# The first gate's modulation on TensorE in four column strips, and the condition spread by a DMA

## The chip, the cores and the metric

One core of a Trainium2 chip runs the whole kernel in one launch. The metric is device time in microseconds (us). The kernel before takes 2292.65 us, the median of three runs (2290.1, 2292.65 and 2293.73). The engines are called by their names or by the profile's: TensorE (PE for matmuls, PEld for weight loads), VectorE (DVE), ScalarE (ACT), GpSimd (POOL) and SyncE (SP), whose queue issues the DMAs here.

## What is computed

Two decoder layers over 256 tokens of 2048 features, all in f32. Each layer is a mixer (a recurrent block, then sparse attention) and a squared-ReLU MLP, so there are four sub-layers s = 0 to 3. Each sub-layer is modulated by a shift, a scale and a gate that come from one condition vector c:

```python
cond = jax.nn.silu(c)
mod = jnp.einsum('bd,jde->bje', cond, ada_w[layer]) + ada_b[layer]
shift, scale, gate = jnp.split(mod, 3, axis=-1)
h = x * (1.0 + scale[:, 0, None]) + shift[:, 0, None]
y = rglru_mixer(h, ...)
x = _layer_norm(DN_ALPHA * x + (1.0 + gate[:, 0, None]) * y, ln_w[layer, 0], ln_b[layer, 0])
```

For one sub-layer, shift, scale and gate are 2048 numbers each, and each is a product of cond (2048) with a 2048 x 2048 block of `ada_w`. The recurrent block projects h to 4096 columns (`lru_in`), applies a short convolution and a gelu, two block-diagonal gate products (`lru_gate`), a scan over the tokens, and an output projection (`lru_out`).

## The kernel before

**Stream of weights.** All large weights come from memory once, as units of 1 MB (128 partitions by 2048 f32) in one fixed order, through a ring of six raw slots (`RAW = 6`). `prefetch` (L95) issues one DMA per unit on SP's queue as soon as a slot is free; `pump` (L109) handles a unit when the builder's own clock says that it has landed (3 us a unit). A unit of kind "w" is split by ScalarE (L135) and VectorE (L136) into a high and a low part, in pieces of 512 columns, that lie in a ring of 16 pieces (`RING`); TensorE then makes each product with three matmuls (`mm3`, L193 to L195). A unit of kind "n" (`lru_gate`) is read by plain f32 matmuls directly from its raw slot (L840, in `gates`).

**Modulation.** A unit of kind "a" is a block of `ada_w` with 128 outputs on the partitions and 2048 inputs along them. VectorE multiplies it by cond and sums along the row in one instruction (L120), which gives 128 of the outputs as a column of `mods[s]`. There are 12 x 16 = 192 of them. For that cond stands on all partitions.

**The condition.** At the start c is loaded as two rows of 1024 on one partition (L291); ScalarE and VectorE make the silu (L314 to L316); a matmul with a column of ones (L319) spreads 512 columns at a time over the partitions, and VectorE copies them out of PSUM (L320).

**The gate.** Once the 16 gate units of a sub-layer are done, `make_gate` (L464) adds the bias and 1 (L466, L467), transposes the columns to rows on TensorE (L470), and stores 2048 numbers to memory (L474); `load_gate` (L477) later loads them onto all partitions. The projection's evacuation multiplies by it (L632).

**Order.** The builder lists the units by hand. The first stage interleaves shift and scale units of sub-layer 0 with the first part of `lru_in`. Then `merge` spreads 24 side units (16 gate units of sub-layer 0, 8 shift and scale units of sub-layer 1) evenly over 36 main units (4 `lru_gate`, 16 `lru_in`, 16 `lru_out`). Of what has been written down, a scheduler then puts each engine's instructions in order.

**PSUM.** Eight banks: four of kind "g" and four of kind "m". A group of `gates` takes two of each. Small tiles of 128 x 512 come from a pool of six (`t2`), larger ones from a pool of twenty (`t4`).

Of the kernel before, what the change touches and what calls it, by code (L numbers as in the profile page):

```python
# [9 lines left out]
F32 = mybir.dt.float32  # L10
# [8 lines left out]
D = 2048  # L19
# [8 lines left out]

C_ADA, C_LNW, C_LNB, C_CW, C_CB, C_GB, C_LAM, C_CMPB, C_N = 0, 192, 256, 320, 384, 400, 432, 448, 450

# [19 lines left out]
class Builder:  # L50
# [18 lines left out]

# [1 line left out]
    def t4(self, shape, dtype=F32):  # L71
# [13 lines left out]

# [1 line left out]
    def set_stream(self, items):  # L87
# [21 lines left out]
    def pump(self):  # L109
        nc = self.nc  # L110
        while self.pi < len(self.items):
            it = self.items[self.pi]
            if it.kind == "d":
                self.pi += 1
                continue
            if self.arrive[self.pi] > self.now:
                return
            r = it.raw
            if it.kind == "a":
                nc.vector.scalar_tensor_tensor(r, r, self.one, self.cond, op0=OP.mult, op1=OP.mult, accum_out=it.col)  # L120
            elif it.kind == "raw":
                if not it.run(r):
                    return
            elif it.kind == "n":
                if not it.done:
                    return
            else:
                w = min(1024, it.width)
                s = it.p0 + 2 * it.group
                if s + 2 > self.cons + RING:  # L130
                    return
                src = r[:, 1024 * it.group:1024 * it.group + w]
                hi = self.whi[:, s % RING:s % RING + 2, :].rearrange("p a b -> p (a b)")[:, :w]
                lo = self.wlo[:, s % RING:s % RING + 2, :].rearrange("p a b -> p (a b)")[:, :w]
                nc.scalar.activation(hi, src, AF.Copy)  # L135
                nc.vector.tensor_tensor(out=lo, in0=src, in1=hi.bitcast(F32), op=OP.subtract)  # L136
                self.prod = s + 2
                it.group += 1
                if 2 * it.group < it.pieces:
                    continue  # L140
            self.pi += 1
            self.inflight -= 1
            self.prefetch()
            if it.then:
                it.then()

# [1 line left out]
    def spawn(self, gen, delay=0.0):  # L148
# [28 lines left out]

# [1 line left out]
    def piece(self, i):  # L179
# [6 lines left out]
    def head(self, kind):  # L186
        """The unit that is next in the stream, as it came."""
        self.until(lambda: self.items[self.pi].kind == kind and not self.items[self.pi].done and self.arrive[self.pi] <= self.now)
        return self.items[self.pi], self.items[self.pi].raw
# [20 lines left out]
    def gemm_ws_outer(self, act, dones, kinds, groups):  # L210
        """Several chunks of columns side by side, a few tiles of the contraction at a time."""
        bs = [[self.bank([128, 2, 256], kind) for _ in range(2)] for kind in kinds]
# [13 lines left out]
    def gemm_as(self, act, done, stagger=None, kind="g"):  # L226
        b = [self.bank([128, 512], kind) for _ in range(2)]
        if not stagger:
# [10 lines left out]
            return  # L239
        # the first token tile runs ahead of the second by as many tiles of weights as the ring holds  # L240
        c0 = self.cons
# [16 lines left out]

# [1 line left out]
    def new_act(self):  # L260
# [17 lines left out]
def build(ctx, tc, a, out):  # L278
# [4 lines left out]

# [1 line left out]
    cond = const.tile([128, 2048], F32, name="cond")  # L285
    B.cond = cond
    B.one = const.tile([128, 1], F32, name="one")
    V.memset(B.one, 1.0)
    crow = B.t4([1, 1024]), B.t4([1, 1024])
    for h in range(2):  # L290
        nc.sync.dma_start(out=crow[h], in_=a["c"][1024 * h:1024 * h + 1024].rearrange("(o n) -> o n", o=1))  # L291
    cols = const.tile([128, C_N], F32, name="cols")
# [15 lines left out]

    # silu(c), on every partition
    ones = const.tile([1, 128], F32, name="ones")  # L310
    V.memset(ones, 1.0)
    for h in range(2):
        cx = B.t4([1, 1024])
        SC.activation(cx, crow[h], AF.Tanh, scale=0.5)  # L314
        V.tensor_scalar(cx, cx, 0.5, 0.5, op0=OP.mult, op1=OP.add)
        V.tensor_tensor(out=cx, in0=cx, in1=crow[h], op=OP.mult)  # L316
        for i in range(2):
            pc = B.bank([128, 512], "m")
            T.matmul(pc, ones, cx[:, 512 * i:512 * i + 512], start=True, stop=True)  # L319
            V.tensor_copy(cond[:, 1024 * h + 512 * i:1024 * h + 512 * i + 512], pc)  # L320

# [1 line left out]
    state = {}  # L323

    def ada_items(s, part, tiles=range(16), then=None):
# [32 lines left out]
    def x_item(g):  # L358
# [6 lines left out]
        return it  # L365

    stream = []
    def w_part(name, ix, k0, k1):
# [16 lines left out]

    stream += merge(lru_in + lru_out, ada_items(0, 2, then=hook(("gate", 0))) + ss_group(*GROUPS1[0]))
    for i, (k0, k1) in enumerate(GROUPS1):
# [29 lines left out]

# [1 line left out]
    def ln_cols(s):  # L419
        return cols[:, C_LNW + 16 * s:C_LNW + 16 * s + 16], cols[:, C_LNB + 16 * s:C_LNB + 16 * s + 16]  # L420

    def make_ss(s, k0=0, k1=16):
        """h = zn * hA + hB, with zn the normalized rows before sub-layer s (its input where s is 0)."""
        m = mods[s]
# [19 lines left out]
    def modulate(s, k0, k1, rows, A):  # L444
        """Up to four feature tiles of the transposed rows become the two parts of the modulated ones."""
        make_ss(s, k0, k1)
# [14 lines left out]

    gate_dram = [B.dram.tile([2048], F32, name=f"gate{s}") for s in range(4)]

# [29 lines left out]

# [1 line left out]
    def split(hi, lo, src):  # L495
        SC.activation(hi, src, AF.Copy)  # L496
        V.tensor_tensor(out=lo, in0=src, in1=hi.bitcast(F32), op=OP.subtract)  # L497

# [1 line left out]
    def residual_source(s):  # L500
# [4 lines left out]
    def ln_task(s, z, t, stats, A, fin=None, rows=None):  # L505
        """Normalizes the rows of token tile t and, with A, makes sub-layer s+1's modulated rows, transposed
        (or with rows, the transposed rows alone; or with fin, the last layer norm's w and b, the output)."""
        mv = B.small([128, 2], "mv")
# [79 lines left out]
    def residual_task(s, z):  # L588
        """The output of sub-layer s, zn w + b, goes to memory until the next layer norm."""
        for n in range(4):  # L590
            w, b = lnrow(s, n)
            yield 3.0
            w, b = (v.rearrange("p (o c) -> p o c", o=1).to_broadcast([128, 2, 512]) for v in (w, b))
            V.tensor_tensor(out=z[n], in0=z[n], in1=w, op=OP.mult)
            V.tensor_tensor(out=z[n], in0=z[n], in1=b, op=OP.add)
            nc.sync.dma_start(out=xd[s][n], in_=z[n])
            yield 1.3
# [4 lines left out]
    def proj(s, A_in, z, A_out, first=True, last=True, fin=None, rows=None, kinds="gggg"):  # L602
        """z += act @ W over four chunks of columns. The last part of a sub-layer applies the gate, adds the
        residual and normalizes."""
        act = B.act_as(A_in)
# [117 lines left out]

    # ================= layer 0: RG-LRU =================
    # softplus(-lambda) from a range-reduced exponential and the series of log1p
    sp2 = const.tile([128, 16], F32, name="sp2")
# [168 lines left out]

    # ================= MLP of layer 0 =================
    B.until(lambda: znT[3] is not None and znT[3][1] == 3)
# [4 lines left out]

    # ================= layer 1: sparse attention =================
    # relative bias by distance: row h, column 127 + distance
    oh = B.t4([33, 512])
# [4 lines left out]

    # compressed keys and values
    kc = const.tile([128, 4, 15], F32, name="kc")
# [4 lines left out]
    def compress(i):  # L917
        """Sixteen of the 32 positions in a block; the other sixteen come with the next unit."""
        j, h = divmod(i, 2)
# [89 lines left out]

    # branch gates  # L1010
    gbank = B.bank([128, 256], "g")
# [26 lines left out]

    # attention
    O = [None] * NK  # L1040
# [8 lines left out]
    def back(t, start, step, n, copies=None):  # L1049
        """The last axis of t walked backwards from start."""  # L1050
        dims = [list(d) for d in t.ap]
# [116 lines left out]

    # ================= MLP of layer 1 =================
    z_in = z  # L1170
# [25 lines left out]
def _layout(i):  # L1196
# [6 lines left out]
    cols = [_cols(f["ada_b"]), _cols(f["ln_w"]), _cols(f["ln_b"]), _cols(f["lru_conv_w"][0]), _cols(f["lru_conv_b"][0]),  # L1203
            _cols(f["lru_gate_b"][0]), _cols(f["lru_lambda"][0]), _cols(f["nsa_cmp_b1"][0])]
    r["cols"] = np.ascontiguousarray(np.concatenate(cols, axis=1))
    r["lnrow"] = np.ascontiguousarray(np.stack([f["ln_w"].reshape(4, D), f["ln_b"].reshape(4, D)], axis=1))
    r["lru_in"] = _units(f["lru_w_in"][0])
# [32 lines left out]
```

## Time and profile before

| | before |
|---|---|
| median of the runs | 2292.65 us |
| lowest and highest run | 2290.1 and 2293.73 us |
| span of the profiled execution | 2292.0 us |
| time of the profiled execution outside its span | none shown |
| TensorE busy | 2198.1 us, 96% |
| VectorE busy | 1672.3 us, 73% |
| ScalarE busy | 1057.2 us, 46% |
| read from memory | 613.30 MB |

The span is the time from the first to the last instruction of one profiled execution. An engine's busy time is the sum of its instructions' time; matmuls are pipelined and their ends are modelled, so spacing from start to start says more than busy time. In a row of the trace, "out<-in" names the tiles (without buffer numbers), and "xN" the number of instructions.

### The profile page before, as it was taken

To read this page: it belongs to the slowest core of one execution; us is meant where nothing else is said; L and a number is where in the kernel's file an instruction comes from. 1 tells how busy PE (TensorE), PEld (TensorE's weight loads), DVE (VectorE), ACT (ScalarE), POOL (GpSimd) and SP (SyncE) were. 2 spreads that over 40 slices of the span, in tenths; PEclk is the share of its full clock that TensorE was granted. 3 is DMA by queue.
4 is the path that set the end of the run, shared out by engine and by line. 5 is a ranking of instruction groups with operands and counts; after the bars stand their busy time and mean duration, and the time that the engine had idled before them with its cause. 6 is when DMAs were issued, how large, how long until landed. Compare 5 with 4: busy or idle time off the path is not lost.

```text
span 2292.0 us, 33881 instructions
## 1 busy us (share of the span) xinstructions
PE 2198.1 (96%) x13970; PEld 1966.2 (86%) x13970; DVE 1672.3 (73%) x1987; ACT 1057.2 (46%) x1383; POOL 0.2 (0%) x4
## 2 busy tenths in 40 slices
PE   4799998989999999999999999999999999999997
PEld 3798977978998998998789988788989989988986
DVE  8899999886777767778887688668766444454456
ACT  2356644364453453444443355536544534443541
POOL 0000000000000000000000000000000000000000
PEclk9899999999999999999999999999999999999999
DMA  9987888988878878788689775356788555555561
GB/s 371 411 331 286 338 328 322 373 346 341 306 302 321 298 273 310 294 302 319 234 292 349 293 272 214 132 192 219 281 308 307 190 190 189 191 184 185 208 250 37
DMA packets 98218, 623.95 MB, mean 272 GB/s; under 512 B 10909, under 2 KB 13405, under 8 KB 26896
## 3 DMA queue, kind: packets, MB, share of 16 engines
q1 hardware_dynamic: 98064, 621.80, 72.5%
q8 instruction: 109, 1.79, 0.3%
q14 instruction: 45, 0.37, 0.0%
HBM read 613.30 MB, written 8.45 MB: 271 GB/s over the span
## 4 chain that ended last, share of the span: by engine, by line
PE 84%; DVE 11%; ACT 2%; issue 2%; DMA 1%; DVEq 0%; SPq 0%; ACTq 0%
PE g L195 26%; PE g L194 26%; PE g L193 26%; DVE raw L120 5%; DVE wlo L136 2%; PE m L1124 1%; PE m L1090 1%; ACT whi L135 1%; DMA raw<-in_lru_in 1%; DVE s L801 1%; PE m L929 1%; PE m L1116 0%; PE m L1127 0%; DVE s L497 0%; ACT s L454 0%
## 5 line engine op out<-in xcount | busy, mean ns | idle before, releaser
L136 DVE TENSOR_TENSOR wlo<-raw,whi 128x1024 fp32r<-128x1024 f32 x721 | 872.1, 1222 | 512.4 <-ACT whi L135 510.9
L135 ACT ACTIVATE whi<-raw 128x1024 fp32r<-128x1024 f32 x721 | 754.7, 1057 | 911.7 <-PE g L195 454.2
L193 PE MATMUL g<-s,whi 128*128 128x256 f32 (+1 forms) x2768 | 781.1, 283 | 51.6 <-ACT s L496 50.0
L194 PE MATMUL g<-s,whi 128*128 128x256 f32 (+1 forms) x2768 | 780.4, 282 | 5.1 <-DVE s L497 5.1
L195 PE MATMUL g<-s,wlo 128*128 128x256 f32 (+1 forms) x2768 | 780.6, 283 | 3.2 <-DVE wlo L136 3.2
L193 PEld LDWEIGHTS g<-s,whi 128*128 128x128 f32 (+1 forms) x2768 | 523.1, 189 | 59.1 <-ACT s L496 53.0
L193 PE MATMUL g<-whi,s 128*128 128x512 f32 x1376 | 547.4, 398 | 5.4 <-ACT s L496 5.4
L194 PE MATMUL g<-wlo,s 128*128 128x512 f32 x1376 | 544.9, 396 | 0.0
L195 PE MATMUL g<-whi,s 128*128 128x512 f32 x1376 | 544.6, 396 | 0.3 <-DVE s L497 0.3
L194 PEld LDWEIGHTS g<-s,whi 128*128 128x128 f32 (+1 forms) x2768 | 525.8, 190 | 8.9 <-DVE s L497 6.8
L195 PEld LDWEIGHTS g<-s,wlo 128*128 128x128 f32 (+1 forms) x2768 | 525.1, 190 | 4.8 <-DVE wlo L136 3.8
L120 DVE SCALAR_TENSOR_TENSOR raw<-raw,one,cond 128x2048 f32<-128x2048 f32 x192 | 447.7, 2345 | 19.1 <-DMA raw<-in_ada 18.9
L193 PEld LDWEIGHTS g<-whi,s 128*128 128x128 f32 x1376 | 258.9, 188 | 70.2 <-ACT s L496 7.4
L195 PEld LDWEIGHTS g<-whi,s 128*128 128x128 f32 x1376 | 258.7, 188 | 64.8 <-DVE s L497 2.2
L194 PEld LDWEIGHTS g<-wlo,s 128*128 128x128 f32 x1376 | 258.9, 188 | 62.0 <-issue 0.8
L454 ACT ACTIVATE s<-s,hB,hA 128x256 f32<-128x256 f32 x32 | 16.7, 590 | 120.9 <-DVE hA L430 80.4
L194 PE MATMUL m<-s,whi 128*128 128x256 f32 x256 | 71.1, 278 | 0.0
L195 PE MATMUL m<-s,wlo 128*128 128x256 f32 x256 | 71.1, 278 | 0.0
L193 PE MATMUL m<-s,whi 128*128 128x256 f32 x256 | 70.8, 279 | 0.2 <-ACT whi L135 0.2
L497 DVE TENSOR_TENSOR s<-t,s 128x512 fp32r<-128x512 f32 x78 | 52.8, 685 | 1.5 <-ACT s L496 1.3
L675 ACT ACTIVATE t<-g 128x512 f32<-128x512 f32 x58 | 33.9, 588 | 34.7 <-PE g L195 34.7
L193 PEld LDWEIGHTS m<-s,whi 128*128 128x128 f32 x256 | 47.8, 188 | 0.5 <-ACT whi L135 0.4
(189 smaller groups left out, 1048.6 us busy)
## 6 DMA issues: line engine op xcount, KB each, us to landing
raw<-in_mlp_w SPq DMA_DIRECT2D x256, 1024.0 KB, 5.0
raw<-in_ada SPq DMA_DIRECT2D x192, 1024.0 KB, 6.6
raw<-in_lru_in SPq DMA_DIRECT2D x28, 1024.0 KB, 8.4
raw<-in_nsa_kv SPq DMA_DIRECT2D x24, 1024.0 KB, 5.3
raw<-in_lru_out SPq DMA_DIRECT2D x16, 1024.0 KB, 6.3
raw<-in_nsa_q SPq DMA_DIRECT2D x16, 1024.0 KB, 6.5
raw<-in_nsa_out SPq DMA_DIRECT2D x16, 1024.0 KB, 4.9
t<-in_lnrow SPq DMA_DIRECT2D x24, 256.0 KB, 6.2
```

The costliest lines, as they stand in the source:

```text
L120: nc.vector.scalar_tensor_tensor(r, r, self.one, self.cond, op0=OP.mult, op1=OP.mult, accum_out=it.col)
L135: nc.scalar.activation(hi, src, AF.Copy)
L136: nc.vector.tensor_tensor(out=lo, in0=src, in1=hi.bitcast(F32), op=OP.subtract)
L193: mm(out, lhi, rhi, start=start, stop=False, skip_group_check=True)
L194: mm(out, lhi, rlo, start=False, stop=False, skip_group_check=True)
L195: mm(out, llo, rhi, start=False, stop=stop, skip_group_check=True)
L497: V.tensor_tensor(out=lo, in0=src, in1=hi.bitcast(F32), op=OP.subtract)
L675: SC.activation(r2, banks[b], AF.Relu)
L801: V.scalar_tensor_tensor(o[:, sh:], p[:, :256 - sh], tap(i, j), o[:, sh:], op0=OP.mult, op1=OP.add)
L929: T.matmul(hv, r[:, 128 * l:128 * l + 128], x[:, :, h:15 + h, l], start=(h == 0 and l == 0), stop=(h == 1 and l == 15))
L1090: T.matmul(ps, qT[:, h, 128 * t:128 * t + 128], kT[g // 2][:, g % 2, :, 0:K], start=True, stop=True)
L1124: T.matmul(po, vt[br][:, kt, 128 * g:128 * g + 128], pT[:, br, kt], start=first, stop=False)
```

## The change

The 16 gate units of sub-layer 0 are replaced by 16 units of the same size in another layout: 128 of the inputs on the partitions, all 2048 outputs along them. Each is multiplied on TensorE straight from its raw slot by four f32 matmuls, whose weights are one column of the condition (`condT`, 128 x 16) and whose outputs are rows of 512 on partitions 0, 32, 64 and 96 of one PSUM bank, summed over the 16 units. Then VectorE adds 1 and the bias on these four partitions, and four DMAs store the gate. The gates of the other three sub-layers stay as they were. The condition is loaded by four DMAs that repeat 512 numbers on all 128 partitions, and its silu is made there, on 128 partitions; the matmuls with ones and the copies go. A second copy of c, with the inputs on the partitions, comes with the column constants (`cols`, 16 columns more).

```diff
-    crow = B.t4([1, 1024]), B.t4([1, 1024])
-    for h in range(2):
-        nc.sync.dma_start(out=crow[h], in_=a["c"][1024 * h:1024 * h + 1024].rearrange("(o n) -> o n", o=1))
+    cd = a["c"]
+    crow = [B.t2([128, 512]) for _ in range(4)]
+    for h in range(4):
+        nc.sync.dma_start(out=crow[h], in_=bass.AP(tensor=cd.tensor, offset=cd.offset + 512 * h, ap=[[0, 128], [1, 512]]))
...
-    ones = const.tile([1, 128], F32, name="ones")
-    V.memset(ones, 1.0)
-    for h in range(2):
-        cx = B.t4([1, 1024])
+    for h in range(4):
+        cx = cond[:, 512 * h:512 * h + 512]
         SC.activation(cx, crow[h], AF.Tanh, scale=0.5)
         V.tensor_scalar(cx, cx, 0.5, 0.5, op0=OP.mult, op1=OP.add)
         V.tensor_tensor(out=cx, in0=cx, in1=crow[h], op=OP.mult)
-        for i in range(2):
-            pc = B.bank([128, 512], "m")
-            T.matmul(pc, ones, cx[:, 512 * i:512 * i + 512], start=True, stop=True)
-            V.tensor_copy(cond[:, 1024 * h + 512 * i:1024 * h + 512 * i + 512], pc)
+    condT = const.tile([128, 16], F32, name="condT")
+    SC.activation(condT, cols[:, C_C:C_C + 16], AF.Tanh, scale=0.5)
+    V.tensor_scalar(condT, condT, 0.5, 0.5, op0=OP.mult, op1=OP.add)
+    V.tensor_tensor(out=condT, in0=condT, in1=cols[:, C_C:C_C + 16], op=OP.mult)
...
+    def gate0_items():
+        acc = []
+        def unit(k):
+            def run(r):
+                if not acc:
+                    acc.append(B.bank([128, 512], "m"))
+                for j in range(4):
+                    T.matmul(acc[0][32 * j:32 * j + 1, :], condT[:, k:k + 1], r[:, 512 * j:512 * j + 512], start=k == 0, stop=k == 15, skip_group_check=True)
+            it = Item("p", a["gate0"][k])
+            it.run = run
+            if k == 15:
+                it.then = lambda: B.spawn(rows())
+            return it
+        def rows():
+            acc_bias = B.t2([128, 512])
+            for j in range(4):
+                nc.sync.dma_start(out=acc_bias[32 * j:32 * j + 1, :], in_=a["gate0_b"][j:j + 1, :])
+            yield 3.0
+            for j in range(4):
+                sl = slice(32 * j, 32 * j + 1)
+                V.scalar_tensor_tensor(acc_bias[sl, :], acc[0][sl, :], 1.0, acc_bias[sl, :], op0=OP.add, op1=OP.add)
+                nc.sync.dma_start(out=gate_dram[0][512 * j:512 * j + 512].rearrange("(o n) -> o n", o=1), in_=acc_bias[sl, :])
+            state["gate", 0] = True
+        return [unit(k) for k in range(NK)]
...
-    stream += merge(lru_in + lru_out, ada_items(0, 2, then=hook(("gate", 0))) + ss_group(*GROUPS1[0]))
+    stream += merge(lru_in + lru_out, gate0_items() + ss_group(*GROUPS1[0]))
```

In `pump`, a unit of the new kind "p" runs its four matmuls when it has landed, in the place where kind "a" issued L120.

## Rows read from the trace of the kernel before

**Rows 1.** The page, part 1: busy time and share of the span.

```profile
PE 2198.1 (96%) x13970; PEld 1966.2 (86%) x13970; DVE 1672.3 (73%) x1987; ACT 1057.2 (46%) x1383; POOL 0.2 (0%) x4
```

**Rows 2.** Busy time by stretch: us, engines, then granted clock, DMA share, GB/s.

```profile
14.00:40.00 26.00, 0.80 (x2) 0.50 (x2) 22.61 (x39) 4.85 (x8) 0.00 (x0) 1.00 1.01 419
40.00:147.00 107.00, 90.25 (x707) 88.65 (x708) 97.36 (x102) 39.61 (x51) 0.00 (x0) 0.92 0.98 387
147.00:304.00 157.00, 150.69 (x1054) 141.02 (x1053) 155.54 (x185) 111.42 (x159) 0.00 (x0) 0.99 0.81 305
```

**Rows 3.** The chain of waits from 147 to 310 us, by line.

```profile
by line: issue 11.1%; DVE raw L120 9.3%; PE g L193 9.2%; PE g L195 9.1%; PE g L194 8.9%; DVE s L801 8.6%; DVE wlo L136 8.4%; DVE s L873 4.4%; DMA raw<-in_lru_out 3.9%; ACT s L850 2.4%; DVE s L870 2.2%; DVE s L868 2.2%; ACT whi L135 1.8%; DV
```

**Rows 4.** Waits of PE, 147 to 374 us: us in total, times, longest us.

```profile
PE g L195 <- DVE wlo L136: 3.2, 3, 2.4
...
PE g L193 <- ACT s L496: 1.4, 1, 1.4
PE g L193 <- ACT s L850: 1.1, 1, 1.1
PE g L193 <- ACT whi L135: 0.5, 1, 0.5
PE m L840 <- DVE s L801: 0.4, 1, 0.4
```

**Rows 5.** Groups of instructions, 147 to 304 us: busy us, mean ns, idle before.

```profile
L120 DVE SCALAR_TENSOR_TENSOR raw<-raw,one,cond 128x2048 f32<-128x2048 f32 x17 | 39.8, 2344 | 0.0
```

**Rows 6.** Timeline of DVE: the last gate unit, the first use of the gate.

```profile
289.24 2.35 DVE L120 SCALAR_TENSOR_TENSOR raw<-raw,one,cond 128x2048 f32<-128x2048 f32 x1
...
314.45 0.68 DVE L632 TENSOR_TENSOR s<-g,s 128x512 f32<-128x512 f32 x1
```

**Rows 7.** PE: timeline (start us, us), source L840 (ns min/median/max), groups by form.

```profile
215.03 1.89 PE L840 MATMUL g<-s,raw 128*128 128x256 f32 x8
...
L840 PE MATMUL g<-s,raw x64: 379/379/380, 154.0 to 278.3; 128*128 128x256 f32 x64
...
L1002 PE MATMUL m<-s,relx 33*16 33x512 f32 x2 | 1.0, 594 | 0.0
...
294.73 0.39 PE L195 MATMUL g<-whi,s 128*128 128x512 f32 x1
...
295.43 0.40 PE L195 MATMUL g<-whi,s 128*128 128x512 f32 x1
295.66 0.28 PE L470 MATMUL m<-ident,g 128*16 128x128 f32 x1
...
296.01 0.40 PE L194 MATMUL g<-wlo,s 128*128 128x512 f32 x1
```

**Rows 8.** DMA issues, 147 to 304 us: KB each, median us to landing.

```profile
raw<-in_ada SPq DMA_DIRECT2D x17, 1024.0 KB, 5.9
```

**Rows 9.** DMA issues, 0 to 45 us.

```profile
raw<-in_ada SPq DMA_DIRECT2D x12, 1024.0 KB, 9.2
```

**Rows 10.** Waits of SP's queue, 0 to 200 us: us in total, times, longest.

```profile
SPq L104 <- PE m L840: 14.2, 2, 13.0
```

**Rows 11.** Timeline of the start: start us, us.

```profile
3.70 2.22 SPq L104 DMA_DIRECT2D raw<-in_ada  x4
...
6.12 7.19 PE L319 MATMUL m<-s,ones 1*128 1x512 f32 x8 [6.12 <-DVE s L316]
...
14.08 2.35 DVE L120 SCALAR_TENSOR_TENSOR raw<-raw,one,cond 128x2048 f32<-128x2048 f32 x1
```

**Rows 12.** Timeline of PE at two times, ten steps from first to last each.

```profile
239.75 0.28 PE L193 MATMUL g<-s,whi 128*128 128x256 f32 x1
...
240.93 0.28 PE L194 MATMUL g<-s,whi 128*128 128x256 f32 x1
...
130.05 0.28 PE L195 MATMUL g<-s,wlo 128*128 128x256 f32 x1
...
131.19 0.28 PE L194 MATMUL g<-s,whi 128*128 128x256 f32 x1
```

More of the change, by code (lines that the diff above doesn't have):

```diff
@@ L27 @@
 GK1 = GK0 * 0.044715
-C_ADA, C_LNW, C_LNB, C_CW, C_CB, C_GB, C_LAM, C_CMPB, C_N = 0, 192, 256, 320, 384, 400, 432, 448, 450
+C_ADA, C_LNW, C_LNB, C_CW, C_CB, C_GB, C_LAM, C_CMPB, C_C, C_N = 0, 192, 256, 320, 384, 400, 432, 448, 450, 466
 RAW = 6
@@ L123, in pump @@
                     return
+            elif it.kind == "p":
+                it.run(r)
             elif it.kind == "n":
@@ L316, in build @@
         V.tensor_tensor(out=cx, in0=cx, in1=crow[h], op=OP.mult)
-        for i in range(2):
-            pc = B.bank([128, 512], "m")
-            T.matmul(pc, ones, cx[:, 512 * i:512 * i + 512], start=True, stop=True)
-            V.tensor_copy(cond[:, 1024 * h + 512 * i:1024 * h + 512 * i + 512], pc)
+    condT = const.tile([128, 16], F32, name="condT")
+    SC.activation(condT, cols[:, C_C:C_C + 16], AF.Tanh, scale=0.5)
+    V.tensor_scalar(condT, condT, 0.5, 0.5, op0=OP.mult, op1=OP.add)
+    V.tensor_tensor(out=condT, in0=condT, in1=cols[:, C_C:C_C + 16], op=OP.mult)
     state = {}
+    gate_dram = [B.dram.tile([2048], F32, name=f"gate{s}") for s in range(4)]
     def ada_items(s, part, tiles=range(16), then=None):
@@ L460, in modulate @@
             A[4 * g + j] = [hi[:, j, :], lo[:, j, :], 3]
-    gate_dram = [B.dram.tile([2048], F32, name=f"gate{s}") for s in range(4)]
     def make_gate(s):
@@ L1203, in _layout @@
     cols = [_cols(f["ada_b"]), _cols(f["ln_w"]), _cols(f["ln_b"]), _cols(f["lru_conv_w"][0]), _cols(f["lru_conv_b"][0]),
-            _cols(f["lru_gate_b"][0]), _cols(f["lru_lambda"][0]), _cols(f["nsa_cmp_b1"][0])]
+            _cols(f["lru_gate_b"][0]), _cols(f["lru_lambda"][0]), _cols(f["nsa_cmp_b1"][0]), _cols(r["c"])]
     r["cols"] = np.ascontiguousarray(np.concatenate(cols, axis=1))
+    r["gate0"] = np.ascontiguousarray(f["ada_w"].reshape(4, NK, 128, 3 * D)[0, :, :, 2 * D:])
+    r["gate0_b"] = np.ascontiguousarray(f["ada_b"].reshape(4, 3 * D)[0, 2 * D:].reshape(4, 512))
     r["lnrow"] = np.ascontiguousarray(np.stack([f["ln_w"].reshape(4, D), f["ln_b"].reshape(4, D)], axis=1))
```

## The prediction

> **What bounds the kernel now.** I read the page first: over the whole run TensorE is busy 96% of the time and VectorE 73% [rows 1]. That average hides the stage in question, so the second view is the table by stretch [rows 2]. The reader is to see there that the change sits in one stretch, 147 to 304 us, the recurrent block's second half: all 16 units of the first gate's modulation are multiplied there, on VectorE. It is busy 155.5 of 157 us, TensorE 150.7, both full. The two stretches before it are another matter: from 14 to 147 us the DMA runs at 0.98 to 1.01 of its engines [rows 2], so memory paces that stage, with VectorE close behind.
>
> Which of the two full engines sets the end of the stage? The chain of waits names both: of 147 to 310 us about a quarter stands at the three matmul lines and as much at VectorE's L120, L801 and L136 [rows 3]. The chain can't decide, since an engine that is never idle is always its own predecessor. What decides is the time in which TensorE truly waited: between 147 and 374 us it is 6.2 us at lines 193 to 195, over six waits [rows 4]. That is all that a less loaded VectorE can hand back to TensorE there, as long as its matmuls run at their pace.
>
> **What is removed.** Sixteen L120 instructions: 17 stand in the stretch, 39.8 us, 2.34 us each; the last of them belongs to the next sub-layer [rows 5], and the last of the gate's starts at 289.2 us [rows 6]. So 37.5 us leave VectorE, 24% of its stage, with the two small sums and the transpose of the old gate. Worth to the end: at most the 6.2 us, because TensorE has no other idle time. I credit all of it.
>
> **What is added on TensorE.** Sixteen units of four matmuls, one column by 512 columns in plain f32, issued when a unit has landed. Each f32 matmul runs as two passes: the records of L840 show eight passes of 256 columns that start 0.216 us apart (1.89 us less the last one's 0.379, over 7) [rows 7]. A pass over 512 columns is then 0.43 us. That a narrow weight makes it no cheaper is seen at L1002, 16 columns of weights by 512: 594 ns a record against 379 for L840's 256, so 0.215 us more for 256 more columns [rows 7]. Alternating with 128-column matmuls costs little: where L470, 16 columns wide, is set between two of them, 0.58 us pass instead of two spacings of 0.233 [rows 7], 0.11 with its own work. I take 0.1 per unit.
>
> Whether passes for different strips run side by side is not shown by any row of before: no two neighbours there go to different strips. So I bound it. Nothing overlaps: 8 passes, 3.46 us a unit, and 16 x 3.56 = 57 us. All strips run at once: the two passes of one strip alone, 0.86 us, and 16 x 0.96 = 15.4 us. Between them lies what an engine does that starts matmuls in order and holds one only while its strip is in use: the second pass of a strip waits for the first, but the first of the next strip may start along with it. Then a unit is 1 + 3 + 1 = 5 passes, 2.16 us, and 16 x 2.26 = 36.2 us. I take this, because records of one engine start in program order throughout the rows, and the program gives both passes of a strip in a row. Next to this: TensorE: Matmul & The Clock Gate of the Trainium skill (Part 3: Packing small matmuls) says that three column tiles of 512 columns ran 2.38 times as fast as one after another. Scaled to four strips that would be an estimate of 2.5 passes a unit, 19 us in all and a time of 2303; no row here shows it.
>
> None of this is hidden. Whatever TensorE gets in this stage lengthens it, since behind each gate matmul stand the matmuls of the main product, in order, and the 16-piece ring of split weights stops the stream when they are late.
>
> **The new waits.** TensorE now waits for a raw unit itself, where VectorE did. A unit of this kind lands a median 5.9 us after its issue in this stage and 9.2 in the first 45 us, where the DMA is fuller [rows 8, 9], and its slot, one of six, is freed only when TensorE has passed the unit. What that can do is seen once: SP waited 13.0 us for L840 to free a slot [rows 10], with all later weight loads queued behind it. Cost: below, nothing; above, a quarter of the 5.9 us at every unit, 1.5 us, 24 us in all. I take 1 us in all, near the lower end: the only matmuls that read a raw unit themselves now, L840's, wait 0.4 us in the whole stage, and that for VectorE [rows 4]. The accumulator keeps one of four "m" banks for the stage; a gate group of the recurrence takes two, so three suffice once the first group's are free.
>
> **The condition.** Four loads of 256 KB replace two of 4 KB at the head of SP's queue. SP issues its first weight load at 3.70 us, and four of its issues take 2.22 us there [rows 11]; two more in front put it near 4.8. One more MB at 419 GB/s [rows 2] is 2.4 us of DMA, part of it in the first 4 us, when little moves. Against it, eight matmul passes and the copies behind them leave: the passes run from 6.12 to 13.31 us, 0.90 us each, twice the 0.43 of the later stage, and the first L120 starts at 14.08 [rows 11]. With four short pairs of VectorE work the condition stands ready near 8 or 9 us, and the first unit lands between 9 and 13 (issue at 4.8, and up to 9.2 to land [rows 9]). So VectorE starts up to 6 us earlier, but the stage until 147 us is paced by the DMA, which gets 2.4 us more to do. Range: 6 us gained to 2 lost; I take 3 gained. The 16-column version of the condition is a few instructions of 0.2 us.
>
> **The gate's end.** Four additions on one partition, four bias loads and four stores instead of one: nine or so SP issues at 0.4 us, and VectorE work of four times at most 0.7 us, beside a VectorE that has just got 37 us back. The gate is first used at 314.5 us, 25 us behind the start of its last unit [rows 6]; that covers it, so nothing. If that cover failed it would be 3 to 5 us once (SP's nine issues).
>
> **The sum**, for the likeliest case: 36.2 - 6.2 + 1 - 3 = +28.0 us on the profiled span of 2292.0, so 2320. The median of the runs is 2292.65, the span 0.65 below it, and nothing else separates them; the time after is 2320 either way. After 374 us nothing is touched: the next stretch starts with the layer norm and its own loads, six slots deep, and can't be fed ahead. No change that can be measured here means within 0.2%, 4.6 us.
>
> **Rivals.** *All four strips at once* (chance 0.23): 15.4 - 6.2 + 1 - 3 = +7, 2299. For it: the strips share neither weights nor output partitions. The Trainium skill's page named above would have it so. Against it: two passes of each strip in a row. *No overlap* (0.22): 57 - 8 = +49, 2341. For it: every neighbouring pair in the trace runs one after another, only nothing there could have done otherwise. *Late units* (0.04): up to 24 us on top of the five-pass sum, 2343. *VectorE set the stage* (0.07), the one that is not slower: the idle time of rows 4 understates what VectorE costs, if it also stretches the matmuls. Their spacing is 0.118 us at 240 us (ten steps in 1.18) and was 0.114 at 130 us [rows 12]. At 0.114 the 150.7 us of TensorE would be 145.6, and room 11.4 instead of 6.2. With strips at once and 6 us at the start: 15.4 - 11.4 - 6 = -2, 2290, and a few less at best. It decides from the point at which the strips' work is under about 17 us; above it no relief of VectorE can pay. Against it: VectorE was nearly as full before 147 us, 97.4 of 107 [rows 2], when the spacing was the shorter one. *Five passes*: 0.44, with its own range from 2311 to 2332.
>
> **Numbers.** Range 2295 to 2345: from the low part of the first rival to nearly the top of the second; outside are the 0.07 of the VectorE case, some 0.04 of the first rival, and some 0.09 above. Faster by over 0.2%: 0.05 (0.03 from VectorE's case, 0.02 from strips at once). Within 0.2%: 0.13 (0.04 and 0.09). Slower: 0.82.
>
> **What would show it.** In the new trace: 176 L120 left of 192, and TensorE records at the new matmul line whose starts within a unit span about 2.2 us (0.9: first rival; 3.5: second). VectorE in the stage down by some 37 us with idle time that waits for TensorE; TensorE without gaps, its wait for `wlo` gone; the stage longer by 28 to 31 us. The first L120 at 9 to 13 us instead of 14.08. I am wrong if the stage ends earlier although TensorE was given work, if the stretch after 374 us changes its length by more than some 3 us, or if TensorE's granted clock falls beside the thin matmuls.

## The result, and the profile after it

The changed kernel takes 2266.61 us (median of four runs, 2258.89 to 2268.39) against 2291.38 us for the kernel before, measured beside it: a ratio of 0.9885, 95% interval 0.9867 to 0.9903 (ratios here and below are of the runs' means). It is 1.15% faster. The prediction said 2320 us and slower; time, range and sign are wrong.

The page of the changed kernel, part 1 [rows 1], says where to look. TensorE has 119 records more and is busy 32.8 us less.

```profile
PE 2165.3 (96%) x14089; PEld 1940.8 (86%) x14089; DVE 1638.9 (72%) x1958; ACT 1058.9 (47%) x1385; POOL 0.2 (0%) x4
```

The stretches of rows 2, and the one that follows them, in the same view (us, then PE, PEld, DVE, ACT, POOL busy, granted clock, DMA share, GB/s):

```profile
14.00:40.00 26.00, 1.00 (x3) 0.71 (x4) 22.40 (x42) 5.67 (x8) 0.00 (x0) 1.00 1.01 422
40.00:147.00 107.00, 91.28 (x715) 89.70 (x716) 97.39 (x103) 39.10 (x50) 0.00 (x0) 0.92 0.99 394
147.00:304.00 157.00, 156.65 (x1154) 133.99 (x1153) 123.97 (x154) 112.50 (x157) 0.00 (x0) 1.00 0.81 304
304.00:374.00 70.00, 70.00 (x315) 57.43 (x314) 61.95 (x77) 27.43 (x30) 0.00 (x0) 1.00 0.84 321
```

In the stage of the change, 147 to 304 us, TensorE is now busy almost without a gap, and VectorE has lost 31.6 us. The first was forecast, for the second some 37. The waits of TensorE from 147 to 374 us [rows 4] are gone but for one:

```profile
PE g L197 <- DVE wlo L138: 0.3, 1, 0.3
```

The strips' matmuls stand at line 379. First the view by source line (duration ns min/median/max, first and last start), then two places of the timeline:

```profile
L379 PE MATMUL m<-raw,condT x128: 590/591/592, 166.9 to 298.1; 128*1 128x512 f32 x128
...
166.86 1.90 PE L379 MATMUL m<-raw,condT 128*1 128x512 f32 x16
168.69 0.39 PE L195 MATMUL g<-s,whi 128*128 128x256 f32 x1
...
174.15 0.28 PE L197 MATMUL g<-s,wlo 128*128 128x256 f32 x1
174.35 1.04 PE L379 MATMUL m<-raw,condT 128*1 128x512 f32 x8
175.32 0.39 PE L195 MATMUL g<-s,whi 128*128 128x256 f32 x1
175.55 0.28 PE L196 MATMUL g<-s,whi 128*128 128x256 f32 x1
```

Eight records of one unit lie within 1.04 us, each 0.59 long; the last starts 0.45 us after the first. That is one pass of 0.43 us and 0.02 for everything else: in the trace four records start from 174.353 to 174.373 us and the other four 0.43 us later, so four strips run their first pass together, then their second. Two units in a row take 168.69 - 166.86 = 1.83 us, 0.915 each. But ten of the 16 units come alone, and each such visit widens the step before and the step behind it as well: from 174.15 to 175.55 are 1.40 us, where two usual steps take 0.23, so a single unit costs 1.17 us. Counted in this way from start to start, all 13 visits cost TensorE 17.8 us. The first rival had 15.4, the forecast 36.2.

With 6.2 us of waits gone the stage should have become some 12 us longer, so where the 25 us came from is not in it. Two rows by source line show it. They hold the matmuls with 512 moving columns, the first of which runs near the end of the stage and the last at the end of the kernel; first the kernel before, then after.

```profile
L193 PE MATMUL g<-whi,s x1376: 388/394/800, 280.1 to 2279.0; 128*128 128x512 f32 x197
```

```profile
L195 PE MATMUL g<-whi,s x1376: 388/392/799, 283.9 to 2250.6; 128*128 128x512 f32 x197
```

The first one starts 3.8 us later than before, the last one 28.4 us earlier. So 32 us were won behind it, nearly all after the stage, where the diff touches nothing. Both kernels issue the same 13,200 matmuls of the split product (the three lines of `mm3`), in the same order but for 132 places between number 866 and 2715, so they can be paired one by one. By that pairing after is 3.6 us late at number 2400 (450 us), 2.6 us ahead at number 6000 (1017 us), and gains until the end. The timeline shows how, at the same matmuls of both (number 10,080 on); before, then after:

```profile
1779.02 0.28 PE L193 MATMUL g<-s,whi 128*128 128x256 f32 x1
1779.13 0.28 PE L194 MATMUL g<-s,whi 128*128 128x256 f32 x1
...
1779.96 0.28 PE L195 MATMUL g<-s,wlo 128*128 128x256 f32 x1
```

```profile
1764.36 0.28 PE L195 MATMUL g<-s,whi 128*128 128x256 f32 x1
1764.47 0.28 PE L196 MATMUL g<-s,whi 128*128 128x256 f32 x1
...
1765.27 0.28 PE L197 MATMUL g<-s,wlo 128*128 128x256 f32 x1
```

From the first to the last row are eight steps, a step being the time from one start to the next: 0.94 us before, 0.91 after. The same for matmuls with 512 columns (number 10,552 on), before and after:

```profile
1839.23 0.39 PE L194 MATMUL g<-wlo,s 128*128 128x512 f32 x1
...
1841.10 0.39 PE L193 MATMUL g<-whi,s 128*128 128x512 f32 x1
```

```profile
1822.47 0.39 PE L196 MATMUL g<-wlo,s 128*128 128x512 f32 x1
...
1824.31 0.39 PE L195 MATMUL g<-whi,s 128*128 128x512 f32 x1
```

Eight steps take 1.87 and 1.84 us. The table by stretch has 102 matmuls more in the same 500 us, at the same granted clock of 1.00 (before, then after):

```profile
1500.00:2000.00 500.00, 498.66 (x3160) 447.58 (x3159) 304.61 (x316) 239.38 (x281) 0.00 (x0) 1.00 0.64 230
```

```profile
1500.00:2000.00 500.00, 498.58 (x3262) 451.24 (x3261) 311.71 (x322) 247.49 (x292) 0.00 (x0) 1.00 0.65 235
```

In this stretch the mean step of neighbours is 117.8 ns before and 113.4 after for 256 columns, 233.3 and 228.9 for 512. It is the same 4.4 ns at either width, so a cost per matmul and not per column. Neither kernel has one pace throughout: before is fast from 110 to 142 us (that is the second half of rows 12) and in a few shorter stretches, and after is slow from 633 to 1204 us for 256 columns, and in shorter ones.

### The profile page after: what moved, and what is told of

Read it like the earlier page. It is cut to its first block, busy times and chain, and to the rows that moved or that the text cites. A ratio compares the mean times of both kernels' runs of the same rounds, so it can differ in the third digit from the quotient of the medians.

```text
span 2263.7 us, 34116 instructions
## 1 busy us (share of the span) xinstructions
PE 2165.3 (96%) x14089; PEld 1940.8 (86%) x14089; DVE 1638.9 (72%) x1958; ACT 1058.9 (47%) x1385; POOL 0.2 (0%) x4
## 4 chain that ended last, share of the span: by engine, by line
PE 87%; DVE 8%; ACT 2%; issue 2%; DMA 1%; DVEq 0%; SPq 0%; ACTq 0%
PE g L196 27%; PE g L195 27%; PE g L197 27%; DVE raw L120 4%; DVE wlo L138 2%; PE m L1155 1%; PE m L1121 1%; ACT whi L137 1%; DMA raw<-in_lru_in 1%; PE m L379 1%; PE m L960 1%; PE g L871 1%; PE m L871 1%; PE m L1147 0%; PE m L1158 0%
## 5 line engine op out<-in xcount | busy, mean ns | idle before, releaser
L195 PE MATMUL g<-whi,s 128*128 128x512 f32 x1376 | 540.8, 393 | 4.2 <-ACT s L527 4.2
L197 PE MATMUL g<-whi,s 128*128 128x512 f32 x1376 | 539.4, 392 | 0.3 <-DVE s L528 0.3
L120 DVE SCALAR_TENSOR_TENSOR raw<-raw,one,cond 128x2048 f32<-128x2048 f32 x176 | 410.2, 2345 | 35.1 <-DMA raw<-in_ada 34.8
```

The source lines that it names most:

```text
L195: mm(out, lhi, rhi, start=start, stop=False, skip_group_check=True)
L197: mm(out, llo, rhi, start=False, stop=stop, skip_group_check=True)
```

## The experiments

The diff does one thing that none of its lines says: it moves tiles in SBUF, the memory on the chip that holds them. `cols` becomes 64 bytes wider, `condT` adds 64, `ones` (512) goes, and the six small tiles (12,288), now asked for first, come ahead of the large ones. The weights' tiles come first and stay; all activations behind them land 11,904 bytes further up, 128 more than a multiple of 256. The first four runs ask whether that is the cause.

**The kernel before, with its activations at after's addresses.**

```
+    first = B.t2([128, 512])
+    V.memset(first[:, 0:1], 0.0)
+    padc = const.tile([128, 32], F32, name="padc")
+    V.memset(padc[:, 0:1], 0.0)
-    ones = const.tile([1, 128], F32, name="ones")
+    ones = B.small([16, 128], "gr", bufs=1)[0:1, :]
```

> The kernel before, with nothing of the change in it; only its activation tiles are moved in SBUF to the byte addresses that they have in the changed kernel (two small unused tiles, and the column of ones in the space of another small tile). Theory 1, placement: the main matmuls (f32r, three per tile) start 4.4 ns apart sooner because of where the activation tiles lie, so 512-column matmuls go from 233.3 to 229 ns and 256-column ones mostly from 118 to 113.5, and the time falls by 30 to 45 us to 2247 to 2262, below the changed kernel's 2266, since the strips' work is missing. Theory 2, the operations: the pace follows from what the change does on TensorE or VectorE; then the pace stays at 233.3 and 118 ns and the time at 2290 to 2294.

Measured: 2257.13 us, ratio 0.9855 [0.9840, 0.9869]. Nothing of the change is in it, and it is faster than after.

**The changed kernel, with its activations moved back** (384 unused bytes ahead of them).

```
+    padc = const.tile([128, 96], F32, name="padc")
+    V.memset(padc[:, 0:1], 0.0)
     cd = a["c"]
```

> The changed kernel with one unused tile of 384 bytes, which puts its activation tiles at the addresses of the kernel before, up to a multiple of 2048 bytes. Theory 1, placement: the pace is 233.3 and 118 ns again, and what is left is the change's own cost, strips 15 us less 6 us of waits: 2296 to 2304, slower than before by 0.2 to 0.5%. Theory 2, the operations: as the changed kernel, 2259 to 2269.

Measured: 2302.07 us, ratio 1.0045 [1.0028, 1.0061]. The whole gain is gone, and what the change's own instructions cost is left. In the view by source line:

```profile
L195 PE MATMUL g<-whi,s x1376: 390/394/796, 286.8 to 2287.3; 128*128 128x512 f32 x197
```

The first matmul of 512 columns is 6.7 us late against before, the last 8.3: the stage's loss is carried to the end.

**The condition alone, and the gate alone,** both edits of the changed kernel and both padded to the old placement. First the condition alone:

```
...
-    stream += merge(lru_in + lru_out, gate0_items() + ss_group(*GROUPS1[0]))
+    stream += merge(lru_in + lru_out, ada_items(0, 2, then=hook(("gate", 0))) + ss_group(*GROUPS1[0]))
```

> Only the condition is spread by DMA; the first gate is made on VectorE as before. Activation tiles at the addresses of the kernel before, up to a multiple of 2048 bytes. Theory 1: pace 233.3 and 118 ns, time 2288 to 2294 (the start is worth 1 us at most). Theory 2, if the eight matmuls with ones at the start set the pace of what follows: pace 229 and 113.5, time 2250 to 2265.

Measured: 2291.74 us, ratio 1.0000 [0.9991, 1.0010]: the condition's spreading is worth nothing. Then the gate alone:

```
...
-        nc.sync.dma_start(out=crow[h], in_=bass.AP(tensor=cd.tensor, offset=cd.offset + 512 * h, ap=[[0, 128], [1, 512]]))
+        nc.sync.dma_start(out=crow[h], in_=a["c"][1024 * h:1024 * h + 1024].rearrange("(o n) -> o n", o=1))
...
+            T.matmul(pc, ones, cx[:, 512 * i:512 * i + 512], start=True, stop=True)
...
```

> Only the first gate goes to TensorE in four strips; the condition is spread by matmuls with ones as before. Activation tiles at the addresses of the kernel before. Theory 1: pace 233.3 and 118 ns, the strips' 15 us less the 6 us of waits, time 2297 to 2304. Theory 2, if the strips set the pace: 229 and 113.5 from about 170 us on, time 2258 to 2270.

Measured: 2300.08 us, ratio 1.0039 [1.0024, 1.0054]. Paired with before it is 1.2 us late at matmul 600 (132 us) and 8.1 at number 1800 (344 us), 6.9 more. Its strips cost 17.8 us, counted as above, so some 11 us came back, and its trace has no wait of TensorE left from 147 to 374 us. That is more than the 6.2 us of rows 4. In part this is so because a wait there counts from the end that is modelled for the matmul before, 0.28 us after its start, while the usual step is 0.118; what the rest is stays open.

**All four matmuls of a unit in one strip**, to see whether it is the strips that make them cheap.

```
-  T.matmul(acc[0][32 * j:32 * j + 1, :], condT[:, k:k + 1], r[:, 512 * j:512 * j + 512], start=k == 0, stop=k == 15, skip_group_check=True)
+  T.matmul(acc[0][0:1, :], condT[:, k:k + 1], r[:, 512 * j:512 * j + 512], start=k == 0 and j == 0, stop=k == 15 and j == 3, skip_group_check=True)
...
```

> After, with the four matmuls of each unit of the first gate all writing the first column strip (output partition 0) instead of four strips; the other three rows of the gate then hold no sums. Addresses as in after. If the strips run side by side because they lie in different column strips (theory 1), the 64 two-pass matmuls go one after the other at the 3.46 us a unit that four rows of before give (8 x 0.432), 55 us in place of the 15 us that after shows, and the run takes about 2267 + 40 = 2307 us. If a matmul with one output row is cheap by itself, whatever strip it writes (theory 2), the unit stays near 0.92 us and the run at 2262 to 2271 us.

Measured: 2307.00 us, ratio 1.0054 [1.0035, 1.0074], which is 40 us over after. Its timeline:

```profile
167.38 4.88 PE L379 MATMUL m<-raw,condT 128*1 128x512 f32 x11
...
172.53 1.88 PE L379 MATMUL m<-raw,condT 128*1 128x512 f32 x4
174.34 0.39 PE L195 MATMUL g<-s,whi 128*128 128x256 f32 x1
```

Eleven records start 0.43 us apart, (4.88 - 0.59) / 10, and two units take 174.34 - 167.38 = 6.96 us. With the same shapes and data, one strip costs 3.48 us a unit and four strips 0.915. The overlap is what the strips give, and it is nearly complete.

**The kernel before, with only the activations 128 bytes further up.** The first run also put the small tiles in another order; this one keeps it.

```
+    padc = const.tile([128, 32], F32, name="padc")
+    V.memset(padc[:, 0:1], 0.0)
     crow = B.t4([1, 1024]), B.t4([1, 1024])
```

> Before, with 128 unused bytes a partition ahead of the activation tiles, so that all of them lie 128 bytes further up, in the order of before; weights stay; nothing of the change. The start of the tiles is then 64 modulo 512, as in after and as in the run of before with moved tiles, but 1088 modulo 2048, not 576. Theory 1 (the offset of the activations sets the pace, and their place modulo 512 is what counts): 113.4 ns a 256-column matmul in most of the run and 2255 to 2270 us. Theory 2 (the order of the tiles or their place modulo 2048 counts): 117.8 ns and 2288 to 2296 us.

Measured: 2260.10 us, ratio 0.9856 [0.9841, 0.9871]. An unused tile of 128 bytes a partition gains 31 us.

**Weights and activations both 128 bytes further up.** The same unused tile, now ahead of the weights' tiles (`raw`, `whi`, `wlo`).

```
+        self.padc = self.const.tile([128, 32], F32, name="padc")
+        nc.vector.memset(self.padc[:, 0:1], 0.0)
...
         self.whi = self.const.tile([128, RING, 512], F32R, name="whi")
```

> Before, with 128 unused bytes a partition ahead of everything, weights and activations alike, so that their distance stays as in before and only the absolute offsets differ. Theory 1 (the offset of the activations alone): as the run with the activations moved by 128 bytes, 2255 to 2270 us. Theory 2 (the distance between the weights' tiles and the activations', which one change moved): as before, 2288 to 2296 us.

Measured: 2292.29 us, ratio 1.0000 [0.9991, 1.0010]. My theory until then, that the activations' own offset counts, fell here: they lie at the very addresses of the run before this one. Its rows at the same matmuls, first of the run with the activations alone moved, then of this one:

```profile
1755.71 0.28 PE L193 MATMUL g<-s,whi 128*128 128x256 f32 x1
...
1756.62 0.28 PE L195 MATMUL g<-s,wlo 128*128 128x256 f32 x1
```

```profile
1777.88 0.28 PE L195 MATMUL g<-s,whi 128*128 128x256 f32 x1
...
1778.82 0.28 PE L197 MATMUL g<-s,wlo 128*128 128x256 f32 x1
```

Eight steps take 0.91 and 0.94 us. What is left is the distance between the two operands of a matmul, weights and activations, and the next runs try that.

**VectorE relieved, at the old placement**, for the rival that VectorE stretches the matmuls.

```
...
-                nc.vector.scalar_tensor_tensor(r, r, self.one, self.cond, op0=OP.mult, op1=OP.mult, accum_out=it.col)
+                w = 64 if it.short else 2048
+                nc.vector.scalar_tensor_tensor(r[:, :w], r[:, :w], self.one, self.cond[:, :w], op0=OP.mult, op1=OP.mult, accum_out=it.col)
...
```

> Before, with VectorE's sums of the first gate taken over 64 of 2048 columns only (most of that gate's sums are left out), so that VectorE loses some 35 of the 37.5 us and TensorE gains no work. Addresses as in before. Theory 1 (what VectorE held up is TensorE's idle time of 147 to 374 us): 2291 - 6 = 2283 to 2287 us, at 117.8 ns. Theory 2 (VectorE's work also stretched TensorE's matmuls, the spacing of 0.118 against 0.114 us): 2280 us or less, with 113.4 ns between 150 and 370 us.

Measured: 2291.78 us, ratio 0.9999 [0.9990, 1.0008]; neither theory's time. In the table by stretch VectorE has become idle for 23.5 us of the stage, and the mean step of the matmuls in it stays 117.8 ns:

```profile
147.00:304.00 157.00, 154.33 (x1075) 144.94 (x1074) 133.51 (x194) 114.69 (x161) 0.00 (x0) 0.99 0.84 323
```

Paired with before, it is 4.9 us ahead at 344 us, and 0.4 at 450. TensorE's waits from 340 to 460 us show where that went; before, then this run:

```profile
PE m L549 <- ACT s L534: 5.9, 2, 3.9
PE g L193 <- ACT s L496: 2.7, 2, 1.7
PE g L194 <- DVE s L497: 2.4, 2, 1.5
```

```profile
PE m L553 <- ACT s L538: 7.5, 1, 7.5
PE g L195 <- ACT s L500: 4.8, 2, 3.2
PE g L196 <- DVE s L501: 2.0, 2, 1.3
```

TensorE reaches the layer norm sooner and waits 3.3 us longer in it, 14.3 in place of 11.0. Coming early can't be all of it, since the run with the gate alone comes 8 us late and waits 12.7 us there; both have matmuls of the stage in another order. VectorE's relief alone is worth 0 to the end all the same, within some 2 us.

**The distance itself.** Four runs of the kernel before with other padding. In the first, weights and activations move, but by different amounts; in the others, the activations alone.

```
+        self.padc = self.const.tile([128, 96], F32, name="padc")
+        nc.vector.memset(self.padc[:, 0:1], 0.0)
...
+    padd = const.tile([128, 32], F32, name="padd")
+    V.memset(padd[:, 0:1], 0.0)
     crow = B.t4([1, 1024]), B.t4([1, 1024])
```

> Before, with 384 unused bytes ahead of the weights' tiles and 128 more between them and the activations: the activations lie 512 bytes further up, the weights 384, and the distance between them grows by 128, as in the run in which the activations alone were moved by 128. Nothing of the change. Theory 1 (the distance between the moving operand's and the stationary operand's tiles sets the pace): 113.4 ns a 256-column matmul over most of the run, 2255 to 2270 us. Theory 2 (the distance counts for nothing by itself; each operand's own place does, so that moving the weights undoes what moving the activations did): 117.8 ns, 2288 to 2296 us.

Measured: 2261.36 us, ratio 0.9871 [0.9854, 0.9887].

```
+    padc = const.tile([128, 16], F32, name="padc")
+    V.memset(padc[:, 0:1], 0.0)
     crow = B.t4([1, 1024]), B.t4([1, 1024])
```

> Before, with the activations alone 64 bytes further up (weights as in before). Theory 1 (distance; a step of 64 bytes is enough to leave the bad distance): 2255 to 2275 us. Theory 2 (the pace goes by whole steps of 128 bytes): as before, 2288 to 2296 us. Neither theory says which; the run maps the effect.

Measured: 2301.90 us, ratio 1.0044 [1.0029, 1.0059]. Slower than before: there is a worse distance than the one that the kernel had.

```
+    padc = const.tile([128, 64], F32, name="padc")
+    V.memset(padc[:, 0:1], 0.0)
```

> Before, with the activations alone 256 bytes further up. If only the distance of before is bad, 2255 to 2270 us; if every second step of 128 bytes is, 2288 to 2296 us, as before.

Measured: 2291.70 us, ratio 0.9997 [0.9988, 1.0006].

```
+    padc = const.tile([128, 128], F32, name="padc")
+    V.memset(padc[:, 0:1], 0.0)
```

> Before, with the activations alone 512 bytes further up, at the same addresses as in the run with weights moved by 384 and activations by 512. If the pace repeats every 512 bytes of distance, 117.8 ns and 2288 to 2296 us, as before; if only the distance of before is bad, or the activations' own addresses count, 2255 to 2270 us.

Measured: 2292.05 us, ratio 1.0000 [0.9991, 1.0009]. Its activations lie where those of the run with weights moved by 384 do; only the weights lie elsewhere, and 31 us lie between the two.

```
+    padc = const.tile([128, 48], F32, name="padc")
+    V.memset(padc[:, 0:1], 0.0)
```

> Before, with the activations alone 192 bytes further up: the last of the four steps of 64 bytes in a period of 256 (the distance between the weights' and the activations' tiles is then a multiple of 256 bytes; 64 more in before, 128 more with the activations moved by 64, 192 more in after and with them moved by 128). If the pace goes by the distance within 256 bytes, a value of its own: 2255 to 2265 us (as at 192) if neighbours within 64 bytes on the other side of the bad distances are alike, 2288 to 2302 us if only 192 is good.

Measured: 2284.80 us, ratio 0.9972 [0.9961, 0.9982]; between the two expectations, a value of its own.

All runs sorted by the distance. It is the start of the activations' tiles less that of `whi`, from the addresses of the compiled kernels, modulo 256 bytes; `wlo` lies a multiple of 256 bytes behind `whi`, and so do the activations behind each other, so that all but 36 of the 13,200 matmuls have the distance of their row. The steps are medians over the trace from 1500 to 2000 us.

```
distance mod 256   kernels (us)                                       step, 256 / 512 columns
 64   before 2291.4; both +128 2292.3; +256 2291.7; +512 2292.1       117 to 118 / 233 ns
      condition alone 2291.7; VectorE relieved 2291.8
      after moved back 2302.1; gate alone 2300.1
128   +64: 2301.9                                                     120 / 232 ns
192   +128: 2260.1; before at after's 2257.1; +384/+512: 2261.4       113 / 229 ns
      after 2266.6; one strip 2307.0
  0   +192: 2284.8                                                    120 / 227 ns
```

Every run falls into its row. Within a row, kernels without the gate's strips differ by at most 4.2 us, while in the row of 192 their activations lie up to 11,776 bytes apart. The same eight steps as above in the run at 128, and in the one at 0, 0.95 and 0.96 us:

```profile
1783.17 0.28 PE L193 MATMUL g<-s,whi 128*128 128x256 f32 x1
...
1784.12 0.28 PE L195 MATMUL g<-s,wlo 128*128 128x256 f32 x1
```

```profile
1771.04 0.28 PE L193 MATMUL g<-s,whi 128*128 128x256 f32 x1
...
1772.00 0.28 PE L195 MATMUL g<-s,wlo 128*128 128x256 f32 x1
```

The best version measured is none of the two kernels compared but the one before with its activations 128 bytes further up: 2257 to 2261 us in its three forms, against 2266.6 for after. With the activations at the same addresses the change's own instructions cost 2266.6 - 2257.1 = 9.5 us.

## Why the prediction was wrong

**The step that failed** is "After 374 us nothing is touched", with its companion in the first part, "as long as its matmuls run at their pace". The operations are indeed untouched, but the tiles they read were moved: 64 bytes of wider `cols` and 64 of `condT` take the distance from 64 to 192 modulo 256, and most of the 13,200 matmuls get a faster pace. The price of that step was set at zero and is -34 us (before against before with moved tiles; 35.5 us for after against after moved back). The prediction did name the sign by which to see it, a change of over 3 us behind 374 us.

**Taken by itself the change is slower, as forecast, but by less.** At the old distance it costs 2302.07 against 2291.22 us, 0.45% [0.28, 0.61]; on the profiled spans 2300.5 - 2292.0 = 8.5 us. The forecast was +28.0, its first rival +7. The mis-sized term is the strips: 36.2 us by five passes a unit, 17.8 measured. The reason given, both passes of a strip in a row hold up the others, does not hold: in the rows of line 379 four passes start together, and the other four when these are through, while in one strip no two start together. The Trainium skill's TensorE: Matmul & The Clock Gate (Part 3: Packing small matmuls) has 2.38 times for three column tiles; here four strips take 0.915 us where one takes 3.48, 3.8 times, so it had the direction right, and the estimate of 19 us scaled from it was near the 17.8.

**VectorE's relief** was credited with all 6.2 us of rows 4, "because TensorE has no other idle time". With the gate in strips some 11 us came back, and 0.3 us of waits are left in the changed kernel; the same view has 2.0 us more before, at L549 in the layer norm, that the prediction left out. But the reason is half of it: with the gate's sums merely shortened, what was won by 344 us went back into the layer norm's wait by 450. That the relief pays here because TensorE has got work to put into the gap fits both runs, but no run shows it by itself.

**The condition**, -3 us with a range of -6 to +2, is 0. The first L120 starts at 12.23 us in place of 14.08 [rows 11], within the forecast 9 to 13, and SP issues the first weights at 5.21 us, later than the 4.8 reckoned:

```profile
5.21 2.66 SPq L104 DMA_DIRECT2D raw<-in_ada  x4
...
12.23 2.35 DVE L120 SCALAR_TENSOR_TENSOR raw<-raw,one,cond 128x2048 f32<-128x2048 f32 x1
```

The first matmul of the split product is 0.8 us earlier than before, and by number 600 (132 us) after is 0.3 us late: the DMA at 0.99 to 1.01 of its engines [rows 2] sets that stage, as the prediction said, so nothing of the earlier start is kept.

**The new waits**, 1 us, are 0 for TensorE: no wait for a raw unit stands among its waits. SP does wait for the strips to free a slot, but in place of other waits. Its waits from 147 to 304 us, before and after:

```profile
SPq L104 <- DVE wlo L136: 74.9, 21, 7.5
SPq L104 <- DVE raw L120: 39.5, 12, 5.3
SPq L104 <- PE m L840: 20.9, 4, 13.0
```

```profile
SPq L104 <- DVE wlo L138: 56.4, 18, 7.1
SPq L104 <- PE m L379: 33.9, 15, 7.6
SPq L104 <- PE m L871: 25.9, 4, 12.5
SPq L104 <- DVE raw L120: 6.9, 1, 6.9
```

**The gate's end** was hidden, as said: no wait of TensorE follows it up to 374 us.

**The rivals.** All strips at once was what happened to the change itself, at 17.8 us in place of 15.4. No overlap and late units did not. "VectorE set the stage" came nearest in time, 2290, for a reason that fell: its clue, 0.118 against 0.114 us a step [rows 12], was the two paces themselves, seen at a place where the kernel before ran the faster one. VectorE has no part in it, since its relief left the step at 117.8 ns. The clue was worth more than the rival made of it: up to 13,200 x 4.4 ns = 58 us hung on it, not the 5 us of one stage.

## What to carry to other kernels

Where an engine is busy 96% of the time with one kind of instruction, a few ns in its step can outweigh an edit (here 4.4 ns gave 34 us, the edit cost 8.5), so look at that step in several places of the trace first; two values in one kernel are worth following up. Tile sizes and unused tiles are part of a change: before crediting or blaming its operations, undo its shift of addresses with a pad, and try some pads on the kernel before. Narrow matmuls belong in different column strips, where four matmuls cost little more than one (here 0.915 us, against 0.86 for the two passes of one).

## What the runs showed of the hardware

- The step of float32r matmuls with 128 x 128 weights depends on the distance between the two operands' tiles in SBUF, with a period of 256 bytes as far as the paddings tried show: 118, 120, 113 and 120 ns for 256 columns at 64, 128, 192 and 0, and 233, 232, 229 and 227 for 512. Steps finer than 64 bytes were not tried. Moving both operands alike changes nothing.
- At one distance the pace can still hold two values. At 192 the step is 113.4 ns in most of the run and 117.8 in stretches of up to hundreds of us (633 to 1204 us in after, other stretches in the runs without the change); at 64 it is the other way round (113 to 114 ns from 110 to 142 us in before); at 128 the levels are 118.7 and 120.0. What turns it stays open; so does the mechanism, of which the runs show only that both operands count and that, between 192 and 64, a matmul loses the same 4.4 ns at either width.
- The plain f32 matmuls did not take part: line 840's (now 871) keep a mean of 215.8 ns a pass of 256 columns in both kernels, and in the runs at 128 and 0.
- Four one-column f32 matmuls of two passes each in four column strips: 0.915 us where two such sets stand in a row, their first passes started together; in one strip, 3.48 us. A set that stands alone among float32r matmuls costs 1.17 us, since the steps before and behind it are wider too.
